# Masks inside the scan, product 1 copied into product 2's bank, head sums side by side, and the attention up-projection by sequence halves

## The chip, the cores and the metric

The kernel runs on one core of one Trainium2 chip. The metric is the device time of one execution in microseconds (us): the median of three runs of the kernel before is 789.84 us (784.76 to 790.59).

## The reference

One layer of a hybrid encoder block on x (1024 x 1024, float32), with one input projection of width 5632 that is cut into nine parts:

```python
h = rmsnorm(x, norm_g[l])
proj = jnp.einsum('bsd,de->bse', h, w_in[l])
q, k, v, z_a, u_b, v_b, z_b, g_a, g_b = jnp.split(proj, pts, axis=-1)
y_a = stick_breaking_attention(q, k, v) * jax.nn.silu(z_a)          # 8 heads of 64
y_b = spatial_gating(gelu(u_b), gelu(v_b), ...) * jax.nn.silu(z_b)  # 8 groups of 64
merged = sigmoid(g_a) * (y_a @ w_up_a) + sigmoid(g_b) * (y_b @ w_up_b)
x = x + merged @ w_out[l]
return rmsnorm(x, final_norm_g)
```

Attention works per head on blocks of 128 queries against all keys up to the block's end:

```python
z = jnp.einsum('bhqd,bhkd->bhqk', qb * scale, kb)
before = s_idx < t_idx                                   # strictly earlier keys only
log_keep = jnp.where(before, jax.nn.log_sigmoid(-z), 0.0)
log_stick = lax.cumsum(log_keep, axis=3, reverse=True) - log_keep
w = jnp.where(before, jnp.exp(jax.nn.log_sigmoid(z) + log_stick), 0.0)
out = jnp.einsum('bhqk,bhkd->bhqd', w, vb)
```

So the weight of key s is sigmoid(z_s) times the product of sigmoid(-z) over the keys between s and the query.

## The kernel before

**A planner orders everything.** Each helper of `Plan` (L90) adds a task with an engine, a cost in us and the tiles that it reads and writes. `issue` (L228) plays the tasks through with those costs, engine by engine, and picks the ready task with the lowest priority number; that order is then the program order of each engine on the chip. For TensorE the priority is the task's number in the program; for the other engines it is the number plus `offset`, so that `ahead(...)` (L796, offset -6000) and the body of `project` (offset -9000) come before attention's work wherever they are ready. Tiles of one tag (`slots`, L347) are handed out strictly in program order: a task can only take a tile of a tag when all earlier tiles of that tag have been taken and a slot is free. The costs are `tt` (L163, elementwise: 0.683 us for 512 columns on VectorE, 1.346 us on GpSimd) and `scan_mult` (L188, 1.207 us for 512 columns).

**Precision.** Every fp32 matrix product is three products of rounded operands (high*high, high*low, low*high). `hi_lo` (L208) splits a tile: ScalarE copies the high part, VectorE (or GpSimd) subtracts to get the low part.

**Stages.** (1) Norm, transposes and v: `make_h`, `v_unit`. (2) Twenty groups of the input projection, `project` (L519), each with two pairs of 128 output columns. A group is a Strassen-type product: seven products of 12 matmuls of 512 columns, from four raw weight tiles and the sums s1 (GpSimd), s2, s4 (VectorE) and s3 (GpSimd), in the PSUM banks Y, Z and X. Product 1 is copied by ScalarE from Y to an SBUF tile p1, product 2 goes to X, and VectorE adds p1 to it; products 5 and 6 are copied out likewise and added to products 7 and 3. The consumers (`make_kq`, `make_za`, `make_gates`, `make_u`, `make_zb`, `make_vb`) finish each of the four results and store it to DRAM. `make_vb` (L748) also runs the spatial mixing in the tiles tr, o, z, r, ak and e, which attention uses too. (3) Attention, `head` (L801): 8 heads in two query halves (`attn_step`, L658) of rows of 512 keys (`attn_row`, L634). For a row, TensorE writes z, ScalarE two sigmoids (keep, beta), and on a diagonal row GpSimd masks both with `causal` (L198); VectorE scans keep from the right, and beta times the scan, shifted by one, is the weight. It is transposed, split and multiplied with v into o. The two halves of o are added, multiplied with the gate path and stored to `y_a` per head. (4) `up` (L853) for the spatial branch (`up_b`, stored as `merged_b`) and, after attention, for the attention branch, both halves of the sequence for each e. (5) The output projection `out_unit` (L939) and the final norm.

**Order of the program** (L806 to L833, L877): kq 0, u 0, zb 0, vb 0, u 1, zb 1, vb 1, za 0, then the eight heads, with the remaining projection groups `ahead` between them: kq 1 and gates 0 after the first head, and so on, gates 7 and `up_b` after the last. The matmuls of these groups fill TensorE wherever those of a head aren't ready.

```python
        if diag:
            pl.causal(keep[:, w - P:w], 1.0)
            pl.causal(beta[:, w - P:w], 0.0)
        else:
            pl.move(keep[:, 512:513], cr)
```

Of the kernel before, what the change touches and what calls it, by code (L numbers as in the profile page):

```python
# [16 lines left out]
P = 128  # L17
# [72 lines left out]
class Plan:  # L90
# [233 lines left out]
def hybrid_block(  # L324
# [22 lines left out]
    slots = {"T": 14, "k": 6, "r": 5, "ak": 4, "e": 4, "f1": 5, "f2": 6, "a": 7, "b": 9, "s": 16,  # L347
# [171 lines left out]
    def project(g, use, keep=False):  # L519
# [26 lines left out]
        y, z = buf("Y"), buf("Z")  # L546
        s1, s2, s4 = buf("a", (P, 4, P)), buf("a", (P, 4, P)), buf("a", (P, 4, P))
# [4 lines left out]
        p1 = buf("f2")  # L552
        pl.copy(p1.all, y.all)
# [36 lines left out]

    def make_kq(p):
        def use(j, half, v, in_psum):
            hi, lo = buf("f2", dt=F32R), buf("f2", dt=F32R)
            pl.hi_lo(hi.all, lo.all, v, "DVE" if in_psum else "POOL")
# [6 lines left out]
    def make_za(a):  # L601
        def use(j, half, v, in_psum):
            t = buf("f2")
            pl.act(t.all, v, AF.Sigmoid)
            pl.tt(t.all, v, t.all, ALU.mult, eng="POOL")
            pl.store(za[2 * a + j][:, half_of(half)], t.all)
        project(ZA + a, use, True)
# [25 lines left out]

    def attn_row(kh, kl, q, i, c, cr):  # L634
# [23 lines left out]
    def attn_step(kh, kl, q, v, p, h, ch):  # L658
# [50 lines left out]
    def make_u(a):  # L709
        def use(j, half, v, in_psum):  # L710
            t = gelu_gate(v)
            pl.tt(t.all, t.all, v, ALU.mult, eng="POOL")
            pl.store(u[2 * a + j][:, half_of(half)], t.all)
        project(U[a], use, True)

    def make_zb(a):
        def use(j, half, v, in_psum):
            t = buf("f1")
            pl.act(t.all, v, AF.Sigmoid)
            pl.tt(t.all, t.all, v, ALU.mult, eng="POOL")  # L720
# [4 lines left out]
        project(ZB[a], use, True)  # L725
# [22 lines left out]
    def make_vb(a):  # L748
        ws = {}

        def use(j, half, v, in_psum):
# [5 lines left out]
            pl.tt(t.all, t.all, v, ALU.mult, eng="DVE" if in_psum else "POOL")  # L757
# [36 lines left out]
        project(VB[a], use, True)  # L794
# [31 lines left out]
    ahead(make_kq, 3)  # L826
    head(2, 1)
    ahead(make_gates, 4)
# [9 lines left out]
    def load_y(br):  # L838
        for half in range(2):
            yh, yl = pair_of()  # L840
            for p in range(4):
                raw = buf("a")
                pl.load(raw.all, (y_a, y_b)[br][p][:, half_of(half)])
                pl.hi_lo(yh[:, p, :], yl[:, p, :], raw.all)
            ys[br, half] = (yh, yl)
# [7 lines left out]
    def up(br, e, tags, use):  # L853
        raw = buf("a", (P, 4, P))
        pl.load(raw.all, w_up[e, br].rearrange("p (k e) -> p k e", e=P))
        w = buf("b", (P, 4, P), F32R), buf("b", (P, 4, P), F32R)
        pl.hi_lo(w[0].all, w[1].all, raw.all)
        for half in range(2):
            t = buf("f2")
            pl.load(t.all, gates[8 * br + e][:, half_of(half)])  # L860
            acc = acc_buf(tags)
            n = 0
            for kt in range(4):
                for a, b in ((0, 0), (0, 1), (1, 0)):
                    pl.mm(acc.all, w[a][:, kt, :], ys[br, half][b][:, kt, :], n == 0, n == 11)
                    n += 1
            pl.tt(t.all, acc.all, t.all, ALU.mult)
            use(half, t)
# [40 lines left out]

    TAGS = ("X", "Y", "Z", "z", "z", "o")  # L910
    for e in range(8):
        def use(half, t):
            fs = half_of(half)
            t1 = buf("f2")
            pl.load(t1.all, merged_b[e][:, fs])
            pl.tt(t.all, t.all, t1.all, ALU.add)
            pl.hi_lo(sub(m_hi[e], fs), sub(m_lo[e], fs), t.all)
        up(0, e, TAGS, use)
# [94 lines left out]
```

## Time and profile before

| what | value |
|---|---|
| median of 3 runs | 789.84 us (784.76 to 790.59) |
| profiled execution, its own time | 789.36 us |
| its span, first to last instruction | 787.6 us |
| mean granted clock of TensorE | 0.990 of full speed |
| instructions | 11035, of them 3524 matmuls |

Busy time counts an engine's instructions as the profile shows them. Matmuls are pipelined, so their shown durations overlap and a busy TensorE (PE) needn't run at its full rate. PEld is the loading of weights into TensorE, DVE is VectorE, ACT is ScalarE, POOL is GpSimd.

### The profile page before, as it was taken

How to read it: one execution, taken by the hardware profiler on the slowest of the kernel's cores; microseconds unless marked ns; L12 is line 12 of the kernel's file. 1: busy time of each engine (PE TensorE's matmuls, PEld its weight loads, DVE VectorE, ACT ScalarE, POOL GpSimd, SP SyncE). 2: the span in 40 equal slices, each digit the busy share in tenths (PEclk: the TensorE clock that was granted, in tenths of full speed). 3: DMA queues.
4: the chain of work that ended last, by engine and by line, in shares of the span. 5: the costliest groups of instructions: out<-in, count | busy, mean ns of one | idle time of the engine just before them, and what ended most of it. 6: DMA issues, size and time to landing. Idle time of an engine off the chain costs nothing. (4 is left out here: it accounts for less than half of the span.)

```text
span 787.6 us, 11035 instructions
## 1 busy us (share of the span) xinstructions
PE 745.3 (95%) x3524; PEld 609.9 (77%) x3524; DVE 585.0 (74%) x814; ACT 424.6 (54%) x852; POOL 394.5 (50%) x426
## 2 busy tenths in 40 slices
PE   4989999998979999999999998999999989999996
PEld 3877877886768887878887786878788868878885
DVE  4869455799578989897989689997988837961132
ACT  6647374646546566766766565666774404331122
POOL 1401647668778969477767568376544100012210
PEclk9999999999989999999999999999999999999999
DMA  9313594322443525545632645543586569980022
GB/s 340 140 54 120 186 243 147 108 95 92 148 147 125 192 97 143 154 136 153 180 103 89 178 131 164 154 128 104 170 264 212 177 203 311 306 306 1 27 80 107
DMA packets 70009, 122.36 MB, mean 155 GB/s; under 512 B 7616, under 2 KB 17344, under 8 KB 69952
## 3 DMA queue, kind: packets, MB, share of 16 engines
q1 hardware_dynamic: 68800, 119.57, 48.3%
q10 hardware_dynamic: 1152, 2.10, 0.7%
q8 instruction: 28, 0.46, 0.2%
q14 instruction: 29, 0.24, 0.1%
HBM read 81.79 MB, written 39.85 MB: 154 GB/s over the span
## 5 line engine op out<-in xcount | busy, mean ns | idle before, releaser
L129 PE MATMUL Y<-T,b 128*128 128x512 f32 x1068 | 286.5, 399 | 4.8 <-ACT f L157 1.7
L129 PEld LDWEIGHTS Y<-T,b 128*128 128x128 f32 x1068 | 196.4, 189 | 45.1 <-ACT f L157 2.6
L129 PE MATMUL Z<-T,b 128*128 128x512 f32 x576 | 159.6, 399 | 5.3 <-DVE b L166 3.2
L166 DVE TENSOR_TENSOR b<-a,b 128x512 fp32r<-128x512 f32 (+1 forms) x120 | 105.8, 883 | 38.7 <-PE Y L129 21.5
L129 PEld LDWEIGHTS Z<-T,b 128*128 128x128 f32 x576 | 105.5, 189 | 26.0 <-DVE b L166 3.6
L157 ACT CAST b<-a 128x512 fp32r<-128x512 f32 (+1 forms) x160 | 97.9, 617 | 42.4 <-PE Y L129 22.2
L166 POOL TENSOR_TENSOR b<-a,b 128x512 fp32r<-128x512 f32 x40 | 64.2, 1606 | 64.5 <-ACT b L157 43.8
L129 PE MATMUL X<-T,b 128*128 128x512 f32 x336 | 90.7, 395 | 0.0
L166 POOL TENSOR_TENSOR f<-f,f 128x512 f32<-128x512 f32 (+1 forms) x44 | 67.7, 1544 | 24.2 <-ACT f L146 14.0
L129 PEld LDWEIGHTS X<-T,b 128*128 128x128 f32 x336 | 62.0, 188 | 12.1
L166 POOL TENSOR_TENSOR a<-a,a 128x512 f32<-128x512 f32 x40 | 63.0, 1575 | 15.0 <-DMA a<-in_w_pairs_dram 6.2
L146 ACT ACTIVATE ak<-z 128x128 f32<-128x128 f32 (+2 forms) x96 | 47.5, 495 | 38.0 <-PE z L129 33.7
L129 PE MATMUL o<-e,k 128*128 128x512 f32 (+1 forms) x192 | 59.9, 350 | 4.2 <-DVE e L166 3.4
L190 DVE TENSOR_TENSOR_SCAN ak<-ak 128x128 f32<-128x128 f32 (+1 forms) x64 | 60.0, 941 | 4.2 <-POOL ak L200 4.2
L129 PE MATMUL z<-k,k 128*128 128x512 f32 (+2 forms) x216 | 59.8, 358 | 3.5 <-DMA k<-d 3.0
L146 ACT ACTIVATE r<-z 128x128 f32<-128x128 f32 (+2 forms) x96 | 47.0, 493 | 26.4 <-PE tr L133 25.8
L166 POOL TENSOR_TENSOR r<-r,ak 128x512 f32<-128x512 f32 x32 | 49.4, 1552 | 22.5 <-DVE ak L190 11.4
L166 DVE TENSOR_TENSOR e<-tr,e 128x512 fp32r<-128x512 f32 (+1 forms) x96 | 51.7, 544 | 9.7 <-ACT e L157 9.6
L133 PE MATMUL tr<-c,r 128*128 128x128 f32 x320 | 56.7, 274 | 0.3 <-DVE e L166 0.2
L157 ACT CAST e<-tr 128x512 fp32r<-128x512 f32 (+1 forms) x96 | 46.0, 480 | 18.2 <-PE tr L133 17.8
L180 POOL TENSOR_SCALAR c<-c 128x1 f32<-128x1 f32 x8 | 1.7, 212 | 107.4 <-ACT f L146 107.4
L166 DVE TENSOR_TENSOR a<-a,a 128x512 f32<-128x512 f32 x40 | 42.0, 1049 | 9.4 <-POOL a L166 6.1
(207 smaller groups left out, 1228.3 us busy)
## 6 DMA issues: line engine op xcount, KB each, us to landing
d<-f SPq DMA_DIRECT2D x112, 256.0 KB, 3.0
a<-in_w_pairs_dram SPq DMA_DIRECT2D x80, 256.0 KB, 2.9
f<-d SPq DMA_DIRECT2D x64, 256.0 KB, 3.6
k<-d SPq DMA_DIRECT2D x48, 256.0 KB, 4.2
k<-in_x_dram SPq DMA_DIRECT2D x8, 512.0 KB, 7.2
d<-b SPq DMA_DIRECT2D x16, 256.0 KB, 2.3
k<-d SPq DMA_DIRECT2D x8, 512.0 KB, 5.9
a<-d SPq DMA_DIRECT2D x16, 256.0 KB, 3.4
```

What stands on the lines that cost most here:

```text
L129: lambda: self.nc.tensor.matmul(out.ap(), lhsT=lhsT.ap(), rhs=rhs.ap(), start=start, stop=stop, **kw),
L133: self.add("PE", 0.109, lambda: self.nc.tensor.transpose(out=out.ap(), in_=in_.ap(), identity=ident.ap()), [out], [in_, ident])
L146: return self.nc.scalar.activation(out=out.ap(), in_=in_.ap(), func=func, scale=sc, **kw)
L157: lambda: self.nc.scalar.copy(out=out.ap(), in_=in_.ap()), [out], [in_])
L166: self.add(eng, cost, lambda: e.tensor_tensor(out=out.ap(), in0=in0.ap(), in1=in1.ap(), op=op), [out], [in0, in1])
L180: self.add(eng, cost, lambda: e.tensor_scalar(out=out.ap(), in0=in0.ap(), scalar1=s1, scalar2=s2, op0=op0, **kw), [out], [in0])
L190: lambda: self.nc.vector.tensor_tensor_scan(out.ap(), in_.ap(), in_.ap(), 1.0 if init is None else init.ap(), op0=ALU.mult, op1=ALU.bypass),
```

## The change

Five things change.

1. **Attention.** The two `causal` masks of a diagonal row go. The scan runs with a second operand, `first_one` (zeros, and an identity in the last 128 columns), as state = max(keep * state, first_one) from 0: the state stays 0 for keys after the query, becomes 1 at it, and is the product before it. One column beside keep is set to 0 on GpSimd. The two one-column copies of the carry move from GpSimd to ScalarE.
2. **Projection.** Product 1 is copied from its bank into the bank of product 2, which accumulates on it; the tile p1 and VectorE's add go. Banks X and Y change roles from group to group. s1, s2 and s4 share one tile. All groups but the gates copy their last result to SBUF (before: all but gates and kq), and the consumers' multiplication runs on VectorE where the operand is in PSUM, else on GpSimd (`near`).
3. **Head sums.** Both heads of a pair write into one tile `os`, one above the other, and the gate is multiplied once per pair and half, 128 partitions on GpSimd; the last pair's sums go to the up-projection without DRAM.
4. **Order.** u 1, zb 1 and vb 1 move behind the first head, `ahead`; kq 1 and gates 0 behind the second; gates 4 one head earlier. The attention up-projection runs by halves: its weights stay resident, and half 0 is `ahead` of half 1.
5. **Planner and slots.** Costs of elementwise operations and scans are raised; f1 has 4 slots (5), b 8 (9), os 2.

The diff, cut to its core:

```diff
     def tt(self, out, in0, in1, op, eng="DVE"):
-        cost = out.n * 0.001042 + 0.15 if eng == "DVE" else out.n * 0.0022 + 0.22
+        near = in0.buf.psum or in1.buf.psum
+        cost = out.n * (0.001042 if near else 0.00135) + 0.15 if eng == "DVE" else out.n * 0.00252 + 0.24
     def scan_mult(self, out, in_, init=None):
-        self.add("DVE", in_.n * 0.001042 * SCAN + 0.14,
+        self.add("DVE", in_.n * 0.00255 + 0.14,
+    def scan(self, out, in_, floor, init):
+        self.add("DVE", in_.n * 0.00255 + 0.14,
+                 lambda: self.nc.vector.tensor_tensor_scan(out.ap(), in_.ap(), floor.ap(), init, op0=ALU.mult,
+                                                           op1=ALU.max), [out], [in_, floor])
...
-        y, z = buf("Y"), buf("Z")
-        s1, s2, s4 = buf("a", (P, 4, P)), buf("a", (P, 4, P)), buf("a", (P, 4, P))
+        groups[0] += 1
+        y, z, xx = buf("XY"[groups[0] % 2]), buf("Z"), buf("YX"[groups[0] % 2])
+        s1 = s2 = s4 = buf("a", (P, 4, P))
...
-        p1 = buf("f2")
-        pl.copy(p1.all, y.all)
+        pl.copy(xx.all, y.all)
...
-        xx = buf("X")
-        product(2, w2, xx, True)
-        pl.tt(p1.all, xx.all, p1.all, ALU.add)
-        after(0, 0, p1.all, False)
+        product(2, w2, xx, False)
+        after(0, 0, xx.all, True)
...
+    def near(in_psum):
+        return "DVE" if in_psum else "POOL"
...
+        edge = keep[:, w:w + 1]
+        kr = keep[:, 0:w].map(lambda a: a[:, ::-1])
         if diag:
-            pl.causal(keep[:, w - P:w], 1.0)
-            pl.causal(beta[:, w - P:w], 0.0)
+            pl.add("POOL", 0.15, lambda: nc.gpsimd.memset(edge.ap(), 0.0), [edge], [])
+            pl.scan(kr, kr, first_one[:, 512 - w:512].map(lambda a: a[:, ::-1]), 0.0)
+            if c == 1:
+                pl.copy(cr, keep[:, 0:1])
         else:
-            pl.move(keep[:, 512:513], cr)
-        kr = keep[:, 0:w].map(lambda a: a[:, ::-1])
-        pl.scan_mult(kr, kr, None if diag else cr)
-        n = w - 1 if diag else w
-        if diag and c == 1:
-            pl.move(cr, keep[:, 0:1])
-        pl.tt(beta[:, 0:n], beta[:, 0:n], keep[:, 1:n + 1], ALU.mult, eng="DVE" if diag else "POOL")
+            pl.copy(edge, cr)
+            pl.scan_mult(kr, kr, cr)
+        pl.tt(beta[:, 0:w], beta[:, 0:w], keep[:, 1:w + 1], ALU.mult, eng="DVE" if diag else "POOL")
...
+        mine, other = slice(64 * h, 64 * h + 64), slice(64 - 64 * h, 128 - 64 * h)
+        pl.copy(os_[mine, :], o[other, :])
+        pl.tt(os_[mine, :], o[mine, :], os_[mine, :], ALU.add)
+        if h == 1:
+            g = buf("f1")
+            pl.load(g.all, za[p][:, half_of(ch)])
+            pl.tt(os_.all, os_.all, g.all, ALU.mult, eng="POOL")
+            if p < 3:
+                pl.store(y_a[p][:, half_of(ch)], os_.all)
...
     make_vb(0)
-    make_u(1)
-    make_zb(1)
-    make_vb(1)
     make_za(0)
     head(0, 0)
+    ahead(make_u, 1)
+    ahead(make_zb, 1)
+    ahead(make_vb, 1)
+    head(0, 1)
     ahead(make_kq, 1)
     ahead(make_gates, 0)
-    head(0, 1)
...
+            if br == 0 and p == 3:
+                raw = sums_of[p, half]
+            else:
                 raw = buf("a")
...
+    wa = [buf("T", QUAD, F32R) for _ in range(4)]
+    wa = [up_weights(0, e, wa[e // 2][:, 2 * (e % 2), :], wa[e // 2][:, 2 * (e % 2) + 1, :]) for e in range(8)]
+    def up_a(half, tags):
+        load_y(0, half)
+        for e in range(8):
+            up(0, e, half, wa[e], tags, merge)
+    ahead(up_a, 0, "XYZ")
+    up_a(1, TAGS)
     for e in range(8):
-        up(0, e, TAGS, use)
         wo_parts(e, 0)
```

## Rows read from the trace of the kernel before

**Rows 1.** The page: span, and busy time by engine.

```profile
span 787.6 us, 11035 instructions
PE 745.3 (95%) x3524; PEld 609.9 (77%) x3524; DVE 585.0 (74%) x814; ACT 424.6 (54%) x852; POOL 394.5 (50%) x426
```

**Rows 2.** Busy time by stretch (from:to, length, busy and instructions by engine, clock).

```profile
core 0: us, PE busy (x) PEld busy (x) DVE busy (x) ACT busy (x) POOL busy (x), PEclk, DMA share, GB/s
0.00:20.00 20.00, 8.73 (x28) 6.72 (x29) 9.12 (x16) 11.82 (x21) 3.06 (x12) 1.00 0.94 342
20.00:80.00 60.00, 56.09 (x267) 45.61 (x266) 47.83 (x84) 35.33 (x77) 13.31 (x14) 1.00 0.29 101
80.00:180.00 100.00, 98.56 (x452) 80.80 (x451) 66.31 (x85) 55.10 (x97) 62.28 (x47) 1.00 0.53 156
180.00:240.00 60.00, 52.45 (x236) 41.83 (x235) 44.36 (x52) 34.91 (x64) 48.11 (x34) 0.94 0.37 123
240.00:640.00 400.00, 391.42 (x1930) 321.24 (x1929) 352.22 (x471) 246.30 (x511) 251.29 (x298) 1.00 0.51 154
640.00:660.00 20.00, 17.64 (x69) 13.79 (x69) 9.78 (x16) 5.88 (x10) 0.00 (x0) 0.91 0.85 271
660.00:700.00 40.00, 39.58 (x174) 32.32 (x173) 35.97 (x60) 17.59 (x31) 0.00 (x0) 1.00 0.93 313
720.00:740.00 20.00, 20.00 (x90) 16.54 (x89) 2.77 (x4) 2.90 (x8) 5.80 (x8) 1.00 0.00 0
```

**Rows 3.** The chain that ended last: gapless stretches of TensorE (start, us, what).

```profile
490.94 0.44 PE tr L133 x4
...
720.63 5.45 PE Z L129 x24
...
776.00 1.94 PE X L129 x16
```

**Rows 4.** The timeline from 210 to 223 us, and TensorE's longest wait from 180 to 640.

```profile
221.56 1.65 PE L129 MATMUL Z<-T,b 128*128 128x512 f32 x3 [3.17 <-DVE b L166]
...
211.54 3.16 POOL L166 TENSOR_TENSOR a<-a,a 128x512 f32<-128x512 f32 x2 [4.09 <-DMA a<-in_w_pairs_dram]
...
219.76 1.75 DVE L166 TENSOR_TENSOR b<-a,b 128x512 fp32r<-128x512 f32 x1
...
PEld o L129 <- DVE e L166: 10.3, 15, 1.9
```

**Rows 5.** The timeline around attention's end, on ScalarE and TensorE.

```profile
632.10 0.58 ACT L157 COPY f<-o 64x512 f32<-64x512 f32 x1 [3.30 <-PE o L129]
645.49 0.62 ACT L157 CAST T<-a 128x512 fp32r<-128x512 f32 x1 [12.80 <-DMA a<-d]
...
646.80 0.73 PE L129 MATMUL o<-T,b 128*128 128x512 f32 x2 [2.27 <-ACT b L157]
```

**Rows 6.** Groups of instructions: busy us, mean ns, idle before them and its releaser.

```profile
L200 POOL TENSOR_SCALAR_AFFINE_SELECT r<-r 128x128 f32<-128x128 f32 x64 | 33.7, 527 | 30.3 <-ACT r L146 29.9
L200 POOL TENSOR_SCALAR_AFFINE_SELECT ak<-ak 128x128 f32<-128x128 f32 x64 | 27.8, 436 | 28.8 <-ACT ak L146 28.7
L196 POOL COPY ak<-c 128x1 f32<-128x1 f32 x32 | 19.2, 607 | 7.4 <-DVE r L166 6.9
L166 DVE TENSOR_TENSOR b<-a,b 128x512 fp32r<-128x512 f32 x116 | 102.2, 882 | 34.5 <-PE Y L129 21.5 <-PE Z L129 7.1 <-ACT b L157 3.1
L166 DVE TENSOR_TENSOR f<-X,f 128x512 f32<-128x512 f32 x28 | 19.1, 681 | 10.8 <-PE X L129 9.5 <-DMA f<-d 1.2
L166 POOL TENSOR_TENSOR f<-f,f 128x512 f32<-128x512 f32 x32 | 48.4, 1519 | 18.7 <-ACT f L146 14.0 <-issue 2.2 <-DMA f<-d 1.4
L166 DVE TENSOR_TENSOR f<-f,f 64x512 f32<-64x512 f32 x16 | 14.5, 908 | 0.4
L190 DVE TENSOR_TENSOR_SCAN ak<-ak,c 128x512 f32<-128x512 f32 x32 | 48.3, 1521 | 0.0
L190 DVE TENSOR_TENSOR_SCAN ak<-ak 128x512 f32<-128x512 f32 x16 | 19.6, 1224 | 0.6 <-POOL ak L200 0.6
```

More of the change, by code (lines that the diff above doesn't have):

```diff
@@ L515, in hybrid_block, with project @@
     T[4] = split_quad(t4_raw)
-    def project(g, use, keep=False):
+    groups = [0]
+    def project(g, use, keep=True):
         use_at, pl.offset = pl.offset, -9000
@@ L593, in use @@
             hi, lo = buf("f2", dt=F32R), buf("f2", dt=F32R)
-            pl.hi_lo(hi.all, lo.all, v, "DVE" if in_psum else "POOL")
+            pl.hi_lo(hi.all, lo.all, v, near(in_psum))
             pl.store(kq_hi[p][j, :, half_of(half)], hi.all)
@@ L604, in use @@
             pl.act(t.all, v, AF.Sigmoid)
-            pl.tt(t.all, v, t.all, ALU.mult, eng="POOL")
+            pl.tt(t.all, v, t.all, ALU.mult, eng=near(in_psum))
             pl.store(za[2 * a + j][:, half_of(half)], t.all)
-        project(ZA + a, use, True)
+        project(ZA + a, use)
     gates = [buf("d", (P, S)) for _ in range(16)]
@@ L711, in use @@
             t = gelu_gate(v)
-            pl.tt(t.all, t.all, v, ALU.mult, eng="POOL")
+            pl.tt(t.all, t.all, v, ALU.mult, eng=near(in_psum))
             pl.store(u[2 * a + j][:, half_of(half)], t.all)
-        project(U[a], use, True)
+        project(U[a], use)
     def make_zb(a):
@@ L719, in use @@
             pl.act(t.all, v, AF.Sigmoid)
-            pl.tt(t.all, t.all, v, ALU.mult, eng="POOL")
+            pl.tt(t.all, t.all, v, ALU.mult, eng=near(in_psum))
             us = buf("f1")
@@ L756, in use @@
             t = gelu_gate(v, "r")
-            pl.tt(t.all, t.all, v, ALU.mult, eng="DVE" if in_psum else "POOL")
+            pl.tt(t.all, t.all, v, ALU.mult, eng=near(in_psum))
             tr = buf("tr")
@@ L826, in hybrid_block @@
     ahead(make_kq, 3)
+    ahead(make_gates, 4)
     head(2, 1)
-    ahead(make_gates, 4)
     ahead(make_gates, 5)
@@ L836, in hybrid_block, with load_y @@
     ys = {}
[L838 to L841, printed above, removed]
+    def load_y(br, half):
+        yh, yl = pair_of()
+        for p in range(4):
+            if br == 0 and p == 3:
+                raw = sums_of[p, half]
+            else:
                 raw = buf("a")
                 pl.load(raw.all, (y_a, y_b)[br][p][:, half_of(half)])
-                pl.hi_lo(yh[:, p, :], yl[:, p, :], raw.all)
-            ys[br, half] = (yh, yl)
+            pl.hi_lo(yh[:, p, :], yl[:, p, :], raw.all)
+        ys[br, half] = (yh, yl)
     accs = [0]
@@ L851, in acc_buf, with up_weights, up, sub @@
         return buf(tags[accs[0] % len(tags)])
-    def up(br, e, tags, use):
+    def up_weights(br, e, hi, lo):
         raw = buf("a", (P, 4, P))
         pl.load(raw.all, w_up[e, br].rearrange("p (k e) -> p k e", e=P))
[L856 to L868, printed above, removed]
+        pl.hi_lo(hi, lo, raw.all)
+        return hi, lo
+    def up(br, e, half, w, tags, use):
+        t = buf("f2")
+        pl.load(t.all, gates[8 * br + e][:, half_of(half)])
+        acc = acc_buf(tags)
+        n = 0
+        for kt in range(4):
+            for a, b in ((0, 0), (0, 1), (1, 0)):
+                pl.mm(acc.all, sub(w[a], slice(kt * P, (kt + 1) * P)), ys[br, half][b][:, kt, :], n == 0, n == 11)
+                n += 1
+        pl.tt(t.all, acc.all, t.all, ALU.mult)
+        use(e, half, t)
+    def sub(v, fs):
+        return View(v.buf, v.idx[:-1] + (fs,)) if len(v.idx) > 1 else v.buf[:, fs]
     merged_b = [buf("d", (P, S)) for _ in range(8)]
     def up_b():
-        load_y(1)
+        for half in range(2):
+            load_y(1, half)
         for e in range(8):
-            up(1, e, "XYZ", lambda half, t: pl.store(merged_b[e][:, half_of(half)], t.all))
+            w = up_weights(1, e, buf("b", (P, 512), F32R).all, buf("b", (P, 512), F32R).all)
+            for half in range(2):
+                up(1, e, half, w, "XYZ", lambda e, half, t: pl.store(merged_b[e][:, half_of(half)], t.all))
     ahead(up_b)
-    load_y(0)
     m_hi, m_lo = [], []
@@ L908, in wo_parts, with merge @@
         wo[c].append((hi, lo))
+    wa = [buf("T", QUAD, F32R) for _ in range(4)]
+    wa = [up_weights(0, e, wa[e // 2][:, 2 * (e % 2), :], wa[e // 2][:, 2 * (e % 2) + 1, :]) for e in range(8)]
+    def merge(e, half, t):
+        fs = half_of(half)
+        t1 = buf("f2")
+        pl.load(t1.all, merged_b[e][:, fs])
+        pl.tt(t.all, t.all, t1.all, ALU.add)
+        pl.hi_lo(sub(m_hi[e], fs), sub(m_lo[e], fs), t.all)
+    def up_a(half, tags):
+        load_y(0, half)
+        for e in range(8):
+            up(0, e, half, wa[e], tags, merge)
     TAGS = ("X", "Y", "Z", "z", "z", "o")
+    ahead(up_a, 0, "XYZ")
+    up_a(1, TAGS)
     for e in range(8):
[L912 to L917, printed above, removed]
-        up(0, e, TAGS, use)
         wo_parts(e, 0)
```

28 lines of the change are left out of this document (12 added, 16 removed).

## The prediction

> **What bounds the kernel now.** I read the page first, then busy time by stretch, the chain that ended last, the timeline of the two worst places, and the groups. The page shows TensorE busy 95% of the span and VectorE 74% [rows 1], which suggests that nothing is left. That busy time overstates, since matmuls overlap. The chain gives the price of one in a gapless run: 24 matmuls of 512 columns in 5.45 us (0.227 each), 16 of 256 in 1.94 (0.121), 4 transposes in 0.44 (0.110) [rows 3]. The code issues 2808 matmuls of 512 columns, 172 of 256, 480 of 128 and 64 of 384 (between 0.121 and 0.227, say 0.174): 637.4 + 20.8 + 52.8 + 11.1 = 722 us. The span is 787.6 [rows 1], so 65.5 us are lost, and the change can only win from these: it removes no matmul.
>
> Where they lie: in 720 to 740 us, without a gap, weight loading is busy 16.54 of 20 us, a share of 0.827 [rows 2]. Dividing each stretch's PEld time by 0.827 gives the time it needs at full rate. Lost are then 11.9 us in 0 to 20 (20 - 6.72/0.827), 4.8 in 20 to 80, 2.3 in 80 to 180, 9.4 in 180 to 240, 11.6 in 240 to 640, 3.3 in 640 to 660, 0.9 in 660 to 700, and 9.7 after the last matmul (776.00 + 1.94 against 787.6). That is 54; the missing 11.5 belong mainly to attention, whose short matmuls need more weight loading for their time than the share allows. So 240 to 640 loses 11.6 to 23; I take 19. The reader should see that start, tail and output projection (29 us of loss before 180 or after 700, which the change hardly touches) are out of reach, and some 32 us (9.4 + 19 + 3.3) are in reach.
>
> Three causes show there. In 180 to 240 GpSimd waits 4.09 us for raw weights before it can form s1; the sums and splits behind it come late, VectorE needs 1.75 us for one split, and TensorE stands still for 3.17 us [rows 4]. The clock is 0.94 there: part of the stretch ran at 1.2 instead of 2.4 GHz [rows 2], worth 0.06 x 60 = 3.6 of the 9.4 us. In attention the waits of weight loading for the split weights e (VectorE's subtraction) sum to 10.3 us, in 15 waits of at most 1.9 [rows 4]: VectorE, busy 396.6 of the 460 us from 180 to 640 [rows 2], runs behind the planned order. After attention, TensorE waits for y: the copy of o begins at 632.10 and the first up-matmul at 646.80, 14.7 us with a store and a load through DRAM between; the filling work covers all but 2.27 us, and the clock then falls to a mean of 0.91 [rows 2, 5].
>
> **Projection.** The 20 adds of p1 go: 20 x 0.681 = 13.6 us of VectorE [rows 6], 15 of them (10.2) behind 180 us. The copy of product 1 stays on ScalarE with a PSUM target; no row shows that, so I bound it by nothing and by one more like the 0.58 of row [rows 5], and count 0 because ScalarE is busy 54% [rows 1]. With the sums in one tile a group takes 5 of the 7 "a" slots instead of all 7, so the next group's raw weights can be loaded while this one runs: the 4.09 us wait should go. Reusing the tile makes s2 wait until s1 is split, which it must be anyway for product 5. Alternating X and Y frees the next group's first bank half a group earlier. What can be late next is xx, held until its consumer has read it (gelu reads it three times), but its next use is the following group's copy. The multiplications that `near` moves to VectorE (8 x 0.681 = 5.4) leave GpSimd 8 x 1.519 = 12.2 [rows 6]. kq's extra copy is four ScalarE operations, hidden likewise. A slot less of b and f1 costs at most some look-ahead; I count nothing, up to 3 us.
>
> **Attention.** 128 masks leave GpSimd, 33.7 + 27.8 = 61.5 us, and 64 one-column copies, of which 32 alone take 19.2 [rows 6]. 64 one-column memsets come instead: between 0 and 0.607 us each [rows 6], I take 0.2 (they need no result, and nothing waits on them but the late product), 13 us, at most 39. GpSimd still loses over 65 of the 299 us that it is busy from 180 to 640 [rows 2]. ScalarE gets the 64 copies: 0 to 0.58 each [rows 5], I take 0.2, 13 us. The added wait is ScalarE's for a scan before it copies the carry; behind it stand the sigmoids of other rows and the high parts of weights. The planner places it when its model has the scan ended, so I count 0, at most 32 x 0.3 = 10 us of ScalarE (0.3 is the scan's measured overrun, 1.521 against 1.224 [rows 6]), which its 46% idle time absorbs. The diagonal path is one engine shorter: the scan follows the sigmoid directly.
>
> Less GpSimd also makes VectorE faster. A split of 512 columns from SBUF takes 0.882 us on average and 1.75 at worst, the same operation with a PSUM operand 0.681; the scans take 1.521 and 1.224 [rows 4, 6]. The excess is 116 x 0.201 + 32 x 0.297 = 32.8 us. With a quarter less GpSimd activity I take 8 back (bounds 0 and 20).
>
> Here a rule speaks against the change. The scan on the diagonal now has a second tensor in SBUF; its row is 1.224 us, the scan beside GpSimd's work 1.521 [rows 6]. The Trainium skill, SBUF — State Buffer, section "Who interferes with whom", says that a VectorE instruction with two SBUF inputs contends with a GpSimd instruction that reads SBUF, not with one that only writes. If the diagonal scan was a one-input case so far, it stretches by 0.297 for 512 columns, and with the shorter ones by 12 us in all, and the forecast below by some 2 us; by the row, the same tile was already given twice, and nothing changes. No run here shows which.
>
> **Head sums and order.** The gate multiplication moves from VectorE (16 x 0.908 = 14.5 us) to GpSimd, 8 x 1.519 = 12.2 [rows 6], behind which only y waits. In the end the path is copy 0.58, add 0.681, multiply 1.519, high part 0.62, low part 0.681 [rows 5, 6]: 4.1 us, with hand-overs 5 to 6 instead of 14.7, and no SP or DMA in it. Half 0 of the attention up-projection, 96 x 0.227 = 21.8 us, is there to cover it. So the 3.3 us go, and a good part of an uncounted us with the clock: gain 4. Weight splits for e 0 to 7 come earlier, 36 VectorE operations with half 0, 36 x 0.681 = 24.5.
>
> u 1, zb 1, vb 1 now run beside attention. VectorE against TensorE's full-rate work, 180 us to attention's end: before 396.6 against 460 - 28.4 = 431.6, or 92%. After 396.6 - 10.2 - 14.5 - 8 + 4 + 24.5 = 392 against 431.6 + 21.8 = 453, or 87%. Its slack grows from 35 to 61 us.
>
> **Planner.** An elementwise operation from SBUF is now planned at 0.841 instead of 0.683 (measured 0.882), on GpSimd at 1.530 instead of 1.346 (measured 1.519), a scan at 1.446 instead of 1.207 (1.224 to 1.521) [rows 6]. TensorE's order is fixed by it, so matmuls of attention should be queued less too early.
>
> **Sum.** 180 to 240: 9.4 us lost, against 2.3 per 100 us in the stretch before with the same kinds of groups [rows 2]; I leave 2, gain 7.4. 240 to 640: 19 lost; VectorE's slack nearly doubles and the plan is truer, so I leave 8, gain 11. End: gain 4. Together 22.4, from the profiled execution's 789.4 us to 767. The three runs' median, 789.84, stands 0.5 above it, so the forecast serves for both.
>
> **Rivals.** (a) All of it goes: 9.4 + 23 + 4, 753 us. Against it: waits for e also come from chance contention, which stays. (b) Little: TensorE's losses are in-order waits, which a fuller mixture doesn't cure, and vb 1 with its 1.75 us operations now sits between two heads whose tiles tr, o, z, r, ak, e are handed out in order. Only the end and most of the weight wait are won, 4 + 3.5: about 782; for it speaks that 88% of VectorE's time in attention is already taken [rows 2]. (c) The other side: VectorE takes work marked `ahead` first, now also vb 1 and half 0 of the up-projection (16 us of multiplications and additions). If fillers are so used up before the last head's second half, that half stands alone. Its 8 rows need, with all eight heads inside the 400 us from 240 to 640 [rows 2], at most 25 us (50 per head), with 8 us of matmuls: 17 us idle, and those 8 at half clock 8 more, 25 in all. Without the gains of 240 to 640 and the end that is 789.4 - 7.4 + 25 = 807; with part of them 800. It decides once fillers end before half 0 of the last head's sums is split; against it, the fillers lasted 12 us beyond attention (632.1 to 644.5) [rows 5] and grow by 22.
>
> **Chances.** Forecast 0.68 (range of its own 757 to 779), (a) 0.11, (b) 0.14, (c) 0.07. Runs of the kernel before lie 5.8 us apart, so 1% is about what a measurement can tell. The range is 752 to 785: it takes in (a), most of (b) and unknown scan, memset and slot costs of 5 us, and leaves out (c) and the upper part of (b). Faster by over 1% (below 781.5): 0.79; within 1%: 0.14; slower: 0.07.
>
> **What would show it.** Right: no wait of GpSimd's sums for raw weights over 2 us, PEld waits for e under 6 us, VectorE busy under 570 us in all, GpSimd under 340, no gap over 1 us between attention's end and the output projection, clock 1.00 from 180 on. Wrong: PEld time per stretch still 3% or more short of 0.827 in attention, VectorE's splits still at 0.88, or a gap in which TensorE waits for the last head.

## The result and the profile after

| | before | after |
|---|---|---|
| median of 4 runs | 790.22 us (784.76 to 790.89) | 766.72 us (766.53 to 766.91) |
| ratio | 1 | 0.972, interval 0.967 to 0.976 |
| span of the profiled execution | 787.6 us | 764.7 us |

The forecast was 767.0 us. One of the four runs of the variant e6 below took 1242.51 us at a granted clock of 0.561, and its median there is that of the other three. The page of after, and busy time by stretch, as in [rows 1, 2]:

```profile
PE 735.0 (96%) x3524; PEld 606.4 (79%) x3524; DVE 575.0 (75%) x788; ACT 433.5 (57%) x920; POOL 308.8 (40%) x298
```

```profile
80.00:180.00 100.00, 100.00 (x461) 83.03 (x462) 66.41 (x88) 59.94 (x106) 63.27 (x47) 1.00 0.56 164
180.00:240.00 60.00, 55.27 (x266) 44.80 (x265) 53.14 (x63) 39.98 (x87) 42.25 (x36) 1.00 0.39 125
240.00:640.00 400.00, 397.52 (x1970) 329.26 (x1969) 348.54 (x458) 254.39 (x565) 171.50 (x168) 1.00 0.56 173
640.00:660.00 20.00, 18.65 (x82) 15.11 (x81) 16.68 (x28) 11.12 (x20) 0.00 (x0) 1.00 0.75 242
```

The prediction's measure (length of a stretch minus PEld / 0.827) shows where TensorE's time came back:

| stretch | lost before | lost after | won | forecast |
|---|---|---|---|---|
| 80 to 180 | 2.3 | -0.4 | 2.7 | 0 |
| 180 to 240 | 9.4 | 5.8 | 3.6 | 7.4 |
| 240 to 640 | 11.6 (19 taken) | 1.9 | 9.7 | 11 |
| 640 to 660 | 3.3 | 1.7 | 1.6 | 4 |
| whole span, against 722 | 65.6 | 42.7 | 22.9 | 22.4 |

The -0.4 only says that the measure is good to half a us. The four stretches make 17.6 of the 22.9 us. Most of the rest can't be placed in a stretch: weight loading itself took 609.9 us before and 606.4 after for the same matmuls, and the measure books these 3.5/0.827 = 4.2 us as work. The sum fits and single terms don't, so the next question is what carried the gain.

These waits and groups of after answer to [rows 4, 6] (the first two: us in total, times, longest us):

```profile
PEld o L129 <- DVE e L167: 5.5, 6, 1.9
POOL a L167 <- DMA a<-in_w_pairs_dram: 5.8, 4, 2.7
L167 DVE TENSOR_TENSOR b<-a,b 128x512 fp32r<-128x512 f32 x108 | 95.7, 887 | 26.3 <-ACT b L157 17.5 <-PE Z L129 3.7 <-POOL b L167 3.2
L191 DVE TENSOR_TENSOR_SCAN ak<-ak,c 128x512 f32<-128x512 f32 x32 | 50.5, 1588 | 0.2
L198 DVE TENSOR_TENSOR_SCAN ak<-ak,c 128x512 f32<-128x512 f32 x16 | 25.0, 1560 | 2.9 <-ACT ak L146 2.9
L167 POOL TENSOR_TENSOR os<-os,f 128x512 f32<-128x512 f32 x8 | 15.2, 1897 | 37.0 <-DVE os L167 36.9
L157 ACT COPY c<-ak 128x1 f32<-128x1 f32 x32 | 6.0, 194 | 5.5 <-DVE ak L198 5.2
```

TensorE's waits for e have halved (10.3 to 5.5 us). But VectorE's operations are no faster: splits 0.887 us (0.882 before), carry scans 1.588 (1.521), diagonal scans of 512 columns 1.560 (1.224). The timelines show why for the splits: in after 56 of the 108 meet no GpSimd instruction but a memset and take 0.682 us on average, the other 52 take 1.109; before, 43 took 0.685 and 73 took 0.999. Fewer splits meet GpSimd's work, but those that do lose more.

### The profile page after: what moved, and what is told of

It is laid out like the page before. It is cut to its first block, busy times and chain, and to the rows that moved or that the text cites. A ratio compares the mean times of both kernels' runs of the same rounds, so it can differ in the third digit from the quotient of the medians.

```text
span 764.7 us, 10791 instructions
## 1 busy us (share of the span) xinstructions
PE 735.0 (96%) x3524; PEld 606.4 (79%) x3524; DVE 575.0 (75%) x788; ACT 433.5 (57%) x920; POOL 308.8 (40%) x298
## 4 chain that ended last, share of the span: by engine, by line
PE 83%; DVE 9%; issue 3%; DMA 2%; ACT 2%; POOL 1%; SPq 0%; POOLq 0%; DVEq 0%; ACTq 0%
PE Y L129 22%; PE X L129 21%; PE Z L129 18%; PE z L129 9%; PE o L129 8%; PE tr L133 5%; DVE b L167 2%; DVE ak L198 1%; DVE ak L191 1%; DMA k<-in_x_dram 1%; DVE e L167 1%; DMA k<-d 1%; DVE T L167 1%; DVE f L167 1%; DVE r L167 1%
## 5 line engine op out<-in xcount | busy, mean ns | idle before, releaser
L129 PE MATMUL Y<-T,b 128*128 128x512 f32 x672 | 180.0, 398 | 1.6 <-ACT b L157 1.3
L129 PE MATMUL X<-T,b 128*128 128x512 f32 x660 | 177.9, 398 | 0.0
L129 PE MATMUL Z<-T,b 128*128 128x512 f32 x540 | 145.2, 397 | 0.0
L129 PEld LDWEIGHTS Y<-T,b 128*128 128x128 f32 x672 | 122.3, 188 | 26.0 <-ACT b L157 1.7
L129 PEld LDWEIGHTS X<-T,b 128*128 128x128 f32 x660 | 119.8, 188 | 22.8 <-POOL b L167 0.4
L129 PEld LDWEIGHTS Z<-T,b 128*128 128x128 f32 x540 | 98.1, 188 | 18.3
L198 DVE TENSOR_TENSOR_SCAN ak<-ak,c 128x128 f32<-128x128 f32 (+1 forms) x64 | 72.8, 1141 | 3.5 <-ACT ak L146 3.4
L167 POOL TENSOR_TENSOR f<-f,f 128x512 f32<-128x512 f32 (+1 forms) x38 | 56.2, 1484 | 36.0 <-ACT f L146 14.7
L146 ACT ACTIVATE r<-z 128x128 f32<-128x128 f32 (+2 forms) x96 | 46.9, 495 | 13.1 <-PE tr L133 12.5
L133 PEld LDWEIGHTS tr<-c,r 128*128 128x128 f32 x320 | 39.9, 140 | 13.6 <-DVE r L167 3.4
L191 DVE TENSOR_TENSOR_SCAN ak<-ak,c 128x512 f32<-128x512 f32 x32 | 50.5, 1588 | 0.2
```

What stands on the lines that cost most here:

```text
L129: lambda: self.nc.tensor.matmul(out.ap(), lhsT=lhsT.ap(), rhs=rhs.ap(), start=start, stop=stop, **kw),
L133: self.add("PE", 0.109, lambda: self.nc.tensor.transpose(out=out.ap(), in_=in_.ap(), identity=ident.ap()), [out], [in_, ident])
L146: return self.nc.scalar.activation(out=out.ap(), in_=in_.ap(), func=func, scale=sc, **kw)
```

## The experiments

Each is the kernel after with one thing changed, except e2, which is the kernel before. "Against after" is the difference of medians. The kernel before, run beside these, had medians of 788.1 to 788.9 us (790.2 beside after); the ratios are against it, and 1 or 2 us in the last column say nothing.

| run | what is changed | median, us | ratio to before (interval) | against after |
|---|---|---|---|---|
| e3 | masks and carry back on GpSimd | 788.00 | 0.999 (0.997 to 1.001) | +21.3 |
| e4 | order of u 1, zb 1, vb 1 and the groups back | 780.17 | 0.989 (0.987 to 0.992) | +13.5 |
| e5 | both back | 786.04 | 0.996 (0.994 to 0.999) | +19.3 |
| e6 | only the 64 carry copies back on GpSimd | 769.03 | 0.975 (0.973 to 0.978) | +2.3 |
| e7 | diagonal scan without a second tensor | 766.23 | 0.972 (0.970 to 0.974) | -0.5 |
| e1 | the planner's old costs | 777.15 | 0.985 (0.983 to 0.988) | +10.4 |
| e8 | planned costs higher | 772.09 | 0.979 (0.977 to 0.981) | +5.4 |
| e9 | planned costs lower | 772.86 | 0.981 (0.977 to 0.984) | +6.1 |
| e10 | e3 with e8's costs | 788.10 | 1.000 (0.998 to 1.001) | +21.4 |
| e2 | kernel before with the new costs | 816.27 | 1.035 (1.032 to 1.037) | |
| e11 | end: DRAM and pairs of halves back | 767.12 | 0.973 (0.970 to 0.977) | +0.4 |
| e12 | projection: p1 and three sums back | 770.15 | 0.976 (0.973 to 0.980) | +3.4 |

### Masks and order

**e3: the masks back on GpSimd.**

```diff
-        edge = keep[:, w:w + 1]
         kr = keep[:, 0:w].map(lambda a: a[:, ::-1])
         if diag:
-            pl.add("POOL", 0.15, lambda: nc.gpsimd.memset(edge.ap(), 0.0), [edge], [])
-            pl.scan(kr, kr, first_one[:, 512 - w:512].map(lambda a: a[:, ::-1]), 0.0)
+            pl.causal(keep[:, w - P:w], 1.0)
+            pl.causal(beta[:, w - P:w], 0.0)
...
-            pl.copy(edge, cr)
+            pl.move(keep[:, 512:513], cr)
```

> The changed kernel with the diagonal masks and the copies of the carry back on GpSimd (128 masks, 64 copies), and the scan without its second tensor. If GpSimd's relief and the shorter diagonal path carry the gain: 775 us or more, and GpSimd busy near 370 us. If they don't: 765 to 769 us, with VectorE's scans on the diagonal back from 1.56 to about 1.22 us for 512 columns.

Measured: 788.0 us, all of the gain gone, with everything else of the change in place. e3's page, its waits of TensorE for e, and the 60 us in which it loses most:

```profile
PE 746.0 (95%) x3524; PEld 613.5 (78%) x3524; DVE 567.5 (72%) x788; ACT 428.3 (54%) x856; POOL 378.7 (48%) x426
PEld o L129 <- DVE e L167: 3.5, 4, 1.3
240.00:300.00 60.00, 50.16 (x227) 39.67 (x227) 45.63 (x62) 33.88 (x63) 40.19 (x31) 0.89 0.38 114
```

The same 60 us in after:

```profile
240.00:300.00 60.00, 59.34 (x295) 49.02 (x294) 51.02 (x69) 36.34 (x67) 37.31 (x28) 1.00 0.53 161
```

e3 loses 12.0 us there (60 - 39.67/0.827), after 0.7. Fewer waits for e (3.5 us against 5.5 in after) don't make it faster, so that sum is a poor measure of the gain. VectorE is busy 45.6 us in the stretch, less than in after: it isn't short of time, it waits. How that begins is in the timelines. GpSimd in e3, then the scans of both kernels (min/median/max ns, first to last start):

```profile
201.29 3.37 POOL L167 TENSOR_TENSOR a<-a,a 128x512 f32<-128x512 f32 x2 [0.63 <-DVE b L167]
204.62 0.54 POOL L206 TENSOR_SCALAR_AFFINE_SELECT ak<-ak 128x128 f32<-128x128 f32 x2
205.12 0.28 POOL L206 TENSOR_SCALAR_AFFINE_SELECT r<-r 128x128 f32<-128x128 f32 x1
205.38 1.28 POOL L167 TENSOR_TENSOR b<-a,b 128x512 fp32r<-128x512 f32 x1
206.63 1.74 POOL L167 TENSOR_TENSOR f<-f,f 128x512 f32<-128x512 f32 x1
...
L191 DVE TENSOR_TENSOR_SCAN ak<-ak,c x32: 1249/1320/2320, 246.1 to 640.4; 128x512 f32<-128x512 f32 x32
...
POOL r L206 <- ACT r L146: 31.9, 17, 8.1
POOL ak L206 <- ACT ak L146: 30.2, 17, 6.8
```

```profile
L198 DVE TENSOR_TENSOR_SCAN ak<-ak,c x64: 409/972/2317, 203.1 to 598.4; 128x128 f32<-128x128 f32 x16, 128x256 f32<-128x256 f32 x16, 128x384 f32<-128x384 f32 x16, 128x512 f32<-128x512 f32 x16
L191 DVE TENSOR_TENSOR_SCAN ak<-ak,c x32: 1252/1339/2307, 231.8 to 611.3; 128x512 f32<-128x512 f32 x32
```

Attention's first z-matmul starts at 198.7 us in e3 and at 198.4 in after. A mask takes 0.28 us here (0.44 and 0.51 on average over e3), but it stands in GpSimd's queue between the group's elementwise operations of 1.3 to 1.7 us each; and for 62 us of e3 (31.9 + 30.2; 58.6 before [rows 6]) GpSimd waits with a mask whose sigmoid isn't ready, and whatever is queued behind it waits too. The scan can't be planned ahead of its mask: the first diagonal scan starts at 212.2 us in e3, 9.1 later than in after (the first masks end at 205.4; VectorE's written order has other work ahead of the scan); the first carry scan at 246.1 against 231.8, the last at 640.4 against 611.3. Meanwhile the work that fills TensorE goes on at its own pace, and from 243.9 to 256.3 us none of it is left in TensorE's order. TensorE in e3, from there:

```profile
246.22 0.44 PE L133 MATMUL tr<-c,r 128*128 128x128 f32 x2 [2.15 <-DVE r L167]
248.50 1.84 PE L129 MATMUL o<-e,k 128*128 128x512 f32 x3 [1.84 <-ACT e L157]
...
285.95 1.38 PE L129 MATMUL o<-e,b 128*128 128x256 f32 x5 [1.09 <-DVE e L167]
293.85 0.97 PE L129 MATMUL X<-T,b 128*128 128x512 f32 x3 [2.09 <-ACT Y L157]
```

The first two lines are a head's chain, the third is the spatial mixing of vb 1 (o from e and b), both without filling work at that moment; in the fourth a group's product waits for ScalarE's copy between two banks.

How much of the delay is GpSimd's queue? Followed row by row through the timelines, a diagonal row of e3 needs 6.9 us on average (64 rows) from the end of its sigmoid to the start of its scan: 1.5 until the mask starts, 0.4 for the mask, and 4.9 from the mask to the scan, behind other work in VectorE's written order. After needs 3.6. So of the 3.2 us more, 2.0 are the mask and its wait in the queue, and 1.3 a later place in VectorE's order.

**e4: the order back.**

```diff
+    make_u(1)
+    make_zb(1)
+    make_vb(1)
     make_za(0)
     head(0, 0)
-    ahead(make_u, 1)
-    ahead(make_zb, 1)
-    ahead(make_vb, 1)
-    head(0, 1)
     ahead(make_kq, 1)
     ahead(make_gates, 0)
+    head(0, 1)
     ahead(make_gates, 1)
```

> The changed kernel with u 1, zb 1 and vb 1 ahead of the first head again, and kq 1 and gates 0 behind it. If mixing them with attention carries the gain of 180 to 240 us: 774 to 778 us, with a wait of over 2 us and a fallen clock before attention starts. If the freed tiles and banks carry it: 766 to 770 us.

Measured: 780.17 us, 2 us above the first branch of the expectation. Rows of e4, a stretch and TensorE in it, then the same stretch of after:

```profile
160.00:200.00 40.00, 32.43 (x142) 25.70 (x141) 29.28 (x39) 21.12 (x37) 26.65 (x20) 0.83 0.26 89
...
178.75 2.16 PE L129 MATMUL o<-e,b 128*128 128x256 f32 x6 [1.16 <-ACT e L157]
185.39 0.58 PE L129 MATMUL o<-e,b 128*128 128x256 f32 x1 [2.17 <-ACT e L157]
```

```profile
160.00:200.00 40.00, 40.00 (x201) 33.63 (x200) 32.32 (x44) 25.57 (x46) 29.89 (x25) 1.00 0.38 126
```

With the old order vb 1's mixing stands before attention, with nothing beside it, and e4 loses 8.9 us there (40 - 25.70/0.827), part of it at a clock of 0.83; after loses nothing. The kernel before, in the same order of groups but with other costs and tiles, lost 4.0 us in these 40.

**e5: both back.** Edits of e3 and e4 together.

> The changed kernel with both undone: masks and carry copies on GpSimd, and u 1, zb 1, vb 1 ahead of the first head. Undone alone, the masks cost 21 us and the order 13.5. If these two are separate gains, the sum is 801 us. If the new order is only good because GpSimd is free (beside attention, masks and the groups' own GpSimd work collide), then the old order is the better one for the old masks: 780 to 788 us, with nothing lost from 240 to 300.

```profile
160.00:200.00 40.00, 32.60 (x143) 25.77 (x142) 29.15 (x38) 21.12 (x37) 26.67 (x20) 0.83 0.28 94
240.00:300.00 60.00, 60.00 (x295) 50.21 (x294) 48.90 (x59) 33.03 (x65) 46.97 (x43) 1.00 0.47 162
```

Measured: 786.04 us. The loss before 200 us is e4's, and the loss of e3 in 240 to 300 isn't there: with the old order u 1, zb 1 and vb 1 have ended, kq 1 and gates fill the first heads, and no second chain stands alone. The four kernels together:

| | masks on GpSimd | masks in the scan |
|---|---|---|
| old order | 786.0 | 780.2 |
| new order | 788.0 | 766.7 |

The new order is worth 13.5 us with the masks in the scan. Without, it costs 2, which is within the spread of those runs (e3 784.7 to 789.5, e5 782.1 to 790.6). The masks are worth 5.9 us in the old order and 21.3 in the new. Neither number belongs to one part. The row-by-row delay moves the same way: 5.3 us in e5 against 3.4 in e4, so 2.0 us a row for the masks in the old order and 3.2 in the new. (It is no price by itself: e9 below has 2.8 and is slower than after.) The 5.9 is no more than a change of the planned costs alone moves (below); only e3 and after were run with other costs as well. All the other parts, without these two, are worth what e5 wins against the kernel before, run beside it: 2.9 us (0.9 to 5.1).

**e6: only the carry copies back.**

```diff
-                pl.copy(cr, keep[:, 0:1])
+                pl.move(cr, keep[:, 0:1])
...
-            pl.copy(edge, cr)
+            pl.move(edge, cr)
```

> The changed kernel with only the 64 one-column copies of the carry back on GpSimd; the masks stay in the scan. If the queue of GpSimd (copies waiting for scans, behind and ahead of 1.5 us multiplications) is what costs, most of the 21 us of the third run come back: 778 us or more. If the 61.5 us of masks cost: 766 to 770 us.

Measured: 769.03 us, +2.3. So of e3's 21.3 us the masks carry nearly all.

**e7: the diagonal scan without its second tensor.** It leaves the causal mask out: the scan's second operand is the tile itself.

```diff
-            pl.scan(kr, kr, first_one[:, 512 - w:512].map(lambda a: a[:, ::-1]), 0.0)
+            pl.scan(kr, kr, kr, 0.0)
```

> The changed kernel with the diagonal scan's second operand being its own input tile instead of the mask tile (so the masks of the diagonal are left out; the output differs in the diagonal blocks). If a second tensor in SBUF stretches the scan, the 512-column scan falls from 1.56 to about 1.25 us, VectorE's busy time by 10 to 12 us, and the time by 0 to 3 us. If the collision with GpSimd's work at that place stretches it, it stays at 1.5 us or more.

```profile
L198 DVE TENSOR_TENSOR_SCAN ak<-ak 128x512 f32<-128x512 f32 x16 | 23.9, 1492 | 2.9 <-ACT ak L146 2.9
```

Measured: 766.23 us, and 1.492 us for the scan against 1.560. The second tensor itself costs nothing, as the timelines show scan by scan: where no GpSimd work but a memset runs beside it, the 512-column scan takes 1.218 us on average in after and 1.217 in e7, eight of 16 scans each. Five scans of after and four of e7 take 2.31 to 2.32 us; beside each of them an elementwise GpSimd operation of 512 columns had begun 0.26 to 0.50 us earlier. The 0.07 us between the two means is that one scan. Where the scan began first, it kept its 1.21 to 1.23 us, and GpSimd's operation took 1.67 to 2.15 where one alone takes 1.29. (One pair of e7 went the other way.) In the kernel before, none of the 16 took over 1.304: beside them ran masks, one-column copies, and one multiplication, which began after the scan. The first scan of 128 columns in after shows the same, 1.52 us where the shortest takes 0.409 (above). The memsets' row is by source (min/median/max ns).

```profile
200.94 3.38 POOL L167 TENSOR_TENSOR a<-a,a 128x512 f32<-128x512 f32 x2 [0.63 <-DVE b L167]
...
203.08 1.52 DVE L198 TENSOR_TENSOR_SCAN ak<-ak,c 128x128 f32<-128x128 f32 x1
...
L664 POOL MEMSET ak<- x64: 89/99/105, 197.6 to 584.7; 128x1 f32 x64
```

The memsets, in contrast, never took over 0.105 us in 64, though 39 of them ran beside a VectorE instruction with two inputs in SBUF. The rule of the Trainium skill that the prediction weighed (SBUF — State Buffer, "Who interferes with whom") agrees on both: GpSimd's elementwise operations read SBUF, its memsets don't. What was wrong was to read the row of 1.224 us as either a one-input case or a settled price: the same tile twice stretches as well, when a GpSimd operation that reads SBUF has begun just before.

### The planner's costs

**e1: old costs.**

```diff
-        near = in0.buf.psum or in1.buf.psum
-        cost = out.n * (0.001042 if near else 0.00135) + 0.15 if eng == "DVE" else out.n * 0.00252 + 0.24
+        cost = out.n * 0.001042 + 0.15 if eng == "DVE" else out.n * 0.0022 + 0.22
...
-        self.add("DVE", in_.n * 0.00255 + 0.14,
+        self.add("DVE", in_.n * 0.001042 * SCAN + 0.14,
```

> The changed kernel with the planner's old costs (elementwise from SBUF 0.683, GpSimd 1.346, scan 1.207 us); the instructions are the same, only their order differs. If the truer plan carries the gain inside attention: about 776 us, and TensorE's waits for e come back towards 10 us. If the order of the groups or the freed GpSimd carries it: 766 to 769 us.

```profile
PEld o L129 <- DVE e L166: 11.3, 13, 2.1
```

Measured: 777.15 us, with TensorE's waits for e back at 11.3 us. Alone this looks like proof that a truer plan matters. **e8 and e9** move the same two numbers past the new ones and part of the way back:

```diff
-        cost = out.n * (0.001042 if near else 0.00135) + 0.15 ...    # e8: 0.00145   e9: 0.00128
-        self.add("DVE", in_.n * 0.00255 + 0.14,                      # e8: 0.0028    e9: 0.0024
```

> The changed kernel with the planner's costs raised once more to the means of its own profile (elementwise from SBUF 0.892, scan 1.574 us for 512 columns). If truer costs always give a better order: 762 to 766 us. If any change of the costs reshuffles the order and the time moves by chance, it lands anywhere within some 10 us of 767, and more likely above.

> The changed kernel with slightly lower planner costs (elementwise from SBUF 0.805, scan 1.369 us for 512 columns), between its own and the old ones. Raising them cost 5.4 us, the old ones 10.4. If the changed kernel's costs are a true optimum: 768 to 772 us, between. If the time moves by chance with any reshuffle of the order: anything from 762 to 778 us.

Measured: 772.09 and 772.86 us. e8's costs (0.892 us for a split, 1.574 for a scan) are nearer to what after measures (0.887, and 1.560 to 1.588) than the change's own (0.841, 1.446), and it is 5.4 us slower. So the same instructions differ by 5 to 6 us from a small change of the planned numbers in either direction, and a difference of that size can be a mere reshuffle of the order. After's own set is the fastest of the four that were run.

**e10: e3 with e8's costs,** to see whether e3 only met an unlucky order.

> The changed kernel with masks and carry copies back on GpSimd, as in the third run (788.0 us), and with the planner's costs of the eighth run (which alone gives 772.1 us). If the masks cost because they block GpSimd's queue beside the groups u 1, zb 1 and vb 1: again 785 us or more, with TensorE losing over 10 us between 200 and 300 us. If the third run was an unlucky order: 770 to 780 us.

```profile
240.00:300.00 60.00, 49.66 (x220) 39.29 (x219) 48.77 (x63) 32.12 (x60) 41.46 (x30) 0.86 0.37 116
```

Measured: 788.10 us, with 12.5 us lost in the same stretch. Against e8 the masks are worth 16.0 us, against after 21.3; either is more than the cost sets alone moved (5 to 10 us).

**e2: the kernel before with the new costs.** The edit is e1's, the other way round.

> The kernel before with the new planner costs alone. If the truer plan carries the gain inside attention: about 780 us. If the other parts carry it: 788 to 791 us.

TensorE in e2 and a stretch of it:

```profile
630.58 0.71 PE L129 MATMUL Y<-T,b 128*128 128x512 f32 x2
...
671.62 1.22 PE L129 MATMUL o<-T,b 128*128 128x512 f32 x2 [8.74 <-ACT b L157]
...
640.00:680.00 40.00, 24.89 (x78) 16.72 (x79) 25.12 (x37) 18.94 (x35) 7.49 (x10) 0.66 0.37 119
```

Measured: 816.27 us, 3.5% slower than before, which neither branch of the expectation had. The last filling matmul is at 630.58, attention ends at 662, and then TensorE waits 8.74 us for the copy through DRAM: the 40 us from 640 on lose 19.8 us, at a clock of 0.66. This is the prediction's rival (c), in another kernel, and with a way through DRAM at its end that (c) doesn't have.

### The end and the projection

**e11: the end as before.**

```diff
-            if p < 3:
-                pl.store(y_a[p][:, half_of(ch)], os_.all)
+            pl.store(y_a[p][:, half_of(ch)], os_.all)
...
-    ahead(up_a, 0, "XYZ")
-    up_a(1, TAGS)
+    load_y(0, 0)
+    load_y(0, 1)
+    for e in range(8):
+        for half in range(2):
+            up(0, e, half, wa[e], TAGS, merge)
```

(and the last pair's sums are loaded from DRAM like the others).

> The changed kernel with the last pair's sums stored to and loaded from DRAM again, and the attention up-projection for both halves of each e after attention (weights still resident). If the end path is worth what was forecast: 769 to 772 us, with a gap of 2 us or more before the up-projection and a fallen clock. If the filling work covers it anyway: 766 to 768 us. If the fillers have run out well before the last head's end: 780 us or more.

```profile
626.08 1.30 PE L129 MATMUL Y<-T,b 128*128 128x512 f32 x5
627.22 2.20 PE L129 MATMUL X<-T,T 128*128 128x512 f32 x9
...
639.23 0.39 PE L129 MATMUL X<-T,T 128*128 128x512 f32 x1
```

Measured: 767.12 us, +0.4. After attention TensorE goes from the spatial branch's matmuls straight to the attention branch's. What covers the way through DRAM are the up-projection's own matmuls that don't need the last sums: the product in X runs nine of its twelve matmuls from 627.22 on, and the other three, which need those sums, from 639.23 on. In e11 TensorE waits nowhere over 1 us between attention and 700 us, and loses 0.2 us in 640 to 660. In after itself one gap remains, while the last y is split:

```profile
650.16 0.96 PE L129 MATMUL Y<-T,T 128*128 128x512 f32 x3 [1.35 <-DVE T L167]
```

**e12: the projection as before.**

```diff
-        s1 = s2 = s4 = buf("a", (P, 4, P))
+        s1, s2, s4 = buf("a", (P, 4, P)), buf("a", (P, 4, P)), buf("a", (P, 4, P))
...
-        pl.copy(xx.all, y.all)
+        p1 = buf("f2")
+        pl.copy(p1.all, y.all)
...
-        product(2, w2, xx, False)
-        after(0, 0, xx.all, True)
+        product(2, w2, xx, True)
+        pl.tt(p1.all, xx.all, p1.all, ALU.add)
+        after(0, 0, p1.all, False)
```

> The changed kernel with product 1 copied to SBUF and added by VectorE again (and its consumer's multiplication on GpSimd), and three tiles for s1, s2 and s4; X and Y still alternate. If the freed weight tiles and VectorE's 13.6 us count as forecast: 772 to 776 us, with waits of GpSimd's sums for raw weights of over 3 us each. If not: 766 to 769 us.

```profile
80.00:180.00 100.00, 98.17 (x452) 80.98 (x451) 68.32 (x86) 58.20 (x102) 71.24 (x52) 1.00 0.54 161
POOL a L167 <- DMA a<-in_w_pairs_dram: 2.9, 3, 1.2
```

Measured: 770.15 us, +3.4, between the expectation's two branches and inside what the cost sets alone move. One piece of it can be told from a reshuffle: in 80 to 180 us, ahead of attention, e12 loses 2.1 us (100 - 80.98/0.827), nearly as before (2.3). After loses nothing there, and so do all the runs that leave projection and order as they are and differ in masks, costs or end alone (e1, e3, e7 to e11). GpSimd's waits for raw weights are shorter with three sum tiles (2.9 us) than in after (5.8), so the freed slots don't explain a gain.

## Why the prediction was right

The time was right because the sum of the losses in reach was about right, and because the change takes most of them. That it came within 0.3 us is luck: the single terms missed by 1.3 to 3.8 us and made it up among themselves, and with neighbouring planned costs the same instructions take 5 to 6 us more. The reasons were only partly right. Of the six signs of being right three came (waits for e, GpSimd, the clock) and three didn't (raw weights, VectorE's 570 us, the gap), and one sign of being wrong came, the splits at 0.887 us.

- **Right.** That nothing went below the 722 us that TensorE needs (no run came near), and that the losses to be had lay mainly between 180 and 660 us (80 to 180 gave 2.7 more). GpSimd under 340 us (308.8), waits for e under 6 (5.5), clock 1.00 from 180 to 740. The attention stretch gave 9.7 us against 11. The one-column copy on ScalarE took 0.194 us against 0.2. Rival (c) is a real mechanism (e2): its uncovered end lost 19.8 us, where 25 were worked out, but 8.74 of them are the way through DRAM, which (c) hadn't counted.
- **Wrong: what the masks do.** The step "the diagonal path is one engine shorter" got no term of the sum; in the new order it is the largest, 16 to 21 us by e3 and e10. The step counted the masks' durations on GpSimd, and not that a mask waits in GpSimd's queue (1.5 us a row in e3) and that its scan then comes later in VectorE's order.
- **Wrong: a sum of independent terms.** Order and masks were priced apart. The table of four shows that some 15 us belong to the two together (21.3 - 5.9), each cell with one set of costs.
- **Wrong: VectorE's slack.** VectorE was to be busy 392 us from 180 to 640; it was 401.7 (53.14 + 348.54), and 575.0 in all, not under 570. The 8 us from less contention didn't come: fewer splits meet GpSimd's work, but each that does takes 1.109 us, where it was 0.999. And slack isn't what decides: in 240 to 300 us e3 has VectorE busy 5.4 us less than after, and loses 11.3 us more on TensorE.
- **Wrong: 180 to 240.** Of the 7.4 us 3.6 came. The wait of 4.09 us for raw weights went (0.6 us of such waits are left in this stretch), but elsewhere others came: over the span they sum to 5.8 us, the longest 2.7, where before it was 6.2, below. And the step overlooked that the new order moves the first head into this stretch (the first carry scan starts at 231.8 us, before at 298.6), and its chain brings stalls of its own. Two lines of before, then TensorE in after:

```profile
POOL a L166 <- DMA a<-in_w_pairs_dram: 6.2, 2, 4.1
L190 DVE TENSOR_TENSOR_SCAN ak<-ak,c x32: 1252/1270/2326, 298.6 to 617.3; 128x512 f32<-128x512 f32 x32
```

```profile
208.91 0.44 PE L133 MATMUL tr<-c,r 128*128 128x128 f32 x2 [1.54 <-DVE r L167]
...
224.25 0.69 PE L129 MATMUL o<-e,k 128*128 128x512 f32 x2 [1.52 <-DVE e L167]
```

- **Not forecast: 80 to 180.** It gave 2.7 us. With the projection as before 2.1 us are lost there again (e12), so the projection's change gives most of it, which the prediction counted with 0 for this stretch. By which of its parts (the copy from bank to bank, or the shared sum tile) stays open.
- **Wrong: the end.** Its 4 us were to come from the way through DRAM; e11 puts 0.4 on that. 640 to 660 lost 1.7 us, with one gap of 1.35 where none over 1 was forecast. The old end, e11, has no such gap; what else covers it (the weights that stay resident, say) wasn't run apart.
- **Not supported: the truer plan.** e1 alone would support it; e8 and e9 show that the two neighbouring sets lose 5 to 6 us, on either side.
- **Small sizes, off.** The memsets took 0.098 us on average against 0.2, the gate multiplication of os 1.897 against 1.519.

Open is by what the planner's orders come out slower with the masks on GpSimd all through attention, not only in its first head: the late scans and the missing filling work are shown, the planner's choice behind them is argued. No run changes the order without the masks' place in the queue, or the other way round, so how the 16 to 21 us divide between the two isn't shown. Of parts worth less than some 5 us in all (e6, e12) the time alone tells nothing.

## What to carry to other kernels

Before long operations of other work are mixed beside a chain that is bound by latency, take the chain's short steps off the in-order queue which that work fills: here 128 steps of 0.28 us and up cost 16 to 21 us of the whole. Try two parts of a change together and apart, since their prices needn't add up. Where a planner fixes the order, run neighbouring sets of costs first, and credit no part with less than they move, unless a stretch of the trace ahead of the reshuffled work shows it.

## What the runs showed of the hardware that was not expected

- Copying 512 columns from one PSUM bank into another takes ScalarE as long as copying them to SBUF:

```profile
L157 ACT COPY Y<-X 128x512 f32<-128x512 f32 x10 | 5.8, 582 | 0.0
L157 ACT COPY f<-Y 128x512 f32<-128x512 f32 x15 | 8.8, 586 | 4.0 <-PE Y L129 4.0
```

- One column costs ScalarE 0.194 us to copy, where GpSimd took 0.607 on average [rows 6]. GpSimd's copies of a column took from 0.177 to 1.112 us in the kernel before, its memsets of one in after from 0.089 to 0.105.
- Where a VectorE scan and an elementwise GpSimd operation met, the one that began later was stretched more: of the diagonal 512-column scans in after, five took 2.31 to 2.32 us beside an operation that had begun before them, and three that began first took 1.21 to 1.23, while GpSimd's operation took 1.67 to 2.14 (1.29 alone). So a mean of 16 says little of the next kernel, in which the two meet elsewhere.
